# One of four chunks of a depthwise convolution, from taps on VectorE to products with tap matrices on TensorE

## The chip, the core and the metric

The kernel runs on one core of a Trainium2 chip. The metric is the device time of one execution in microseconds (us). The kernel before takes 2749.17 us (median of three runs, 2747.8 to 2751.32). The engines are named as the profile names them: PE is TensorE (its weight loads are PEld), DVE is VectorE, ACT is ScalarE, POOL is GpSimd, SP is SyncE. POOL and SP issue most DMAs here, each in its own order.

## What is computed

One step of a two-layer encoder trunk, for a prompt of 1024 frames and 8 running streams of 16 frames, 1152 columns in all, everything in fp32. Layer 0 mixes in two ways side by side: stick-breaking attention over 8 heads, and a convolution module. Only the second is touched. It takes 512 channels through a gated projection, a depthwise convolution of 31 taps over time, a layernorm over channels and a SiLU:

```python
u = a * jax.nn.sigmoid(g)
u_ext = jnp.pad(u, ((0, 0), (CONV_STATE, 0), (0, 0)))
y = lax.conv_general_dilated(u_ext, dw_w[:, None, :], window_strides=(1,), padding='VALID',
    feature_group_count=CONV_CH) + dw_b
c_out = jax.nn.silu(layernorm(y, ln_g, ln_b))
out = jnp.concatenate([a_out, c_out], axis=-1) @ w_out
```

For the running streams, the 30 cached rows of each stream stand ahead of its 16 new ones.

## The kernel before, in words

Channels lie on the 128 partitions, time in the free dimension, so that the 512 channels are four chunks (0 to 3). `mixer0` runs layer 0's mixer. `start` does the first projections; then comes a loop over four pairs of heads, p = 0 to 3, called here the first to the fourth pair. While one pair's attention runs (`attend`), the projections of the next (`proj`) fill PE, and the gate and value of a conv chunk (`ag`) stand among them: chunk 2 in the first pair, chunk 3 in the second. Chunks 0 and 1 are made in `start`.

`gate` and `value` evacuate the two projections into a tile `u` of 30 + 1024 columns for the prompt and 8 blocks of 46 for the streams. `tap(c, j)` is one of the 31 taps of chunk c: two DVE instructions, y += w[j] * u shifted by j, one over the 1024 prompt columns and one over the 128 stream columns. So there are 124 taps. `TAPS` deals them: 26 beside the first projections, 36, 38 and 24 beside the first, second and third pair. After the 31st tap a chunk is written to `cat_d` in DRAM. `conv_norm`, beside the fourth pair, loads the four chunks by column group (`yl`, three groups g of 384 columns) and does the layernorm; its mean is a product with ones (`mu`).

In `attend`, each block of 128 queries gives scores z on PE, two sigmoids on ACT (`sg`, `kp`), a scan over `kp` on DVE (L907) and a product into `sg` on DVE (L909); then PE transposes `sg` (`tpa`, L388) and multiplies with the values (`ava`). A score block is written z p i q: z217 is the third pair's second head, last query block, and sg217 the tile that follows from it.

Three lists set the order: the attention's steps with the projections by `merge` (by PE cost, with lags), the taps among them by `level` (by DVE cost), and then the framework places each engine's instructions by a cost model of its own. At run time each engine takes its instructions strictly in that order, and so do the DMA queues of SP and POOL. Where the fourth pair begins, tiles `cr` bring the attention's finished rows back from `cat_d` (SP, L1062), ACT and DVE split them into `cat`, and the output projection `psoa` reads them.

Of the kernel before, what the change touches and what calls it, by code (L numbers as in the profile page):

```python
# [15 lines left out]
P = 128  # L16
# [4 lines left out]
TAPS = (26, 36, 38, 24)  # L21
# [10 lines left out]
UW = UP + 8 * US  # L32
NF = 32
# [91 lines left out]
def tile_trunk(ctx, tc, ins, outs):  # L125
# [26 lines left out]
    dw = const.tile([P, 4, CW], F32, name="dw")  # L152
    cvec = const.tile([P, 3, 4], F32, name="cvec")
    for t, n in ((norms, "norms"), (dw, "dw"), (cvec, "cvec")):
        (nc.scalar.dma_start if n == "norms" else put)(t, ins[n])
# [23 lines left out]
    xr_d = [dram.tile([KC, P, T], F32, name=f"xr_d{l}") for l in range(2)]  # L179
    hb_d = [dram.tile([7, NF // 2, P, TW], F32, name=f"hb_d{l}") for l in range(2)]  # L180
# [474 lines left out]
    def mixer0():  # L655
        with ExitStack() as st:
# [16 lines left out]
            for p in range(4):  # L673
                mine = [p, 4 + p, 8 + p]
                if 1 <= p < 3:
                    mine[1:1] = [16 + p + 1, 12 + p + 1]
                order += mine
# [8 lines left out]
            us, ys, tapped = {}, {}, [0] * 4  # L686
            conv_pool = ExitStack()
            cv = Bufs(conv_pool.enter_context(pool("conv")), u=2, y=1)

            def gate(c, ps, g):  # L690
                if g == 0:
                    assert c < 2 or tapped[c - 2] == CW
                    us[c] = cv.tile([P, UW], F32, "u", f"u{c}")
                    nc.gpsimd.memset(us[c][:, 0:CW - 1], 0.0)
                    dma(us[c][:, UP:].rearrange("p (b t) -> p b t", t=US)[:, :, 0:CW - 1], ins["conv_in"][:, c])
# [8 lines left out]
            def u_parts(c, ps, g):  # L704
                n = G if g < 2 else TP - 2 * G
                o = CW - 1 + g * G
                parts = [(us[c][:, o:o + n], ps[:, :n], rstd[g][:, :n])]
                if g == 2:
                    parts.append((us[c][:, UP:].rearrange("p (b t) -> p b t", t=US)[:, :, CW - 1:],
                                  ps[:, n:G].rearrange("p (b t) -> p b t", t=16), None))  # L710
                return parts

            def value(c, ps, g):
                for dst, src, _ in u_parts(c, ps, g):
                    tt(dst, src, dst, ALU.mult)
                if g == 2:
                    put(outs["conv_p"][c], us[c][:, TP:UP])
                    put(outs["conv_s"][c], us[c][:, UP:].rearrange("p (b t) -> p b t", t=US)[:, :, 16:])

            def tap(c, j):  # L720
                if j == 0:
# [5 lines left out]
                          u[:, UP:].rearrange("p (b t) -> p b t", t=US)[:, :, j:j + 16]))  # L727
# [13 lines left out]
            taps = [Step(0.0, lambda c=c, j=j: tap(c, j), 1340.0) for c in range(4) for j in range(CW)]  # L741
# [220 lines left out]
            vs = pp.tile([P, 8, 2, HD], F32, "vs", "vs0")  # L962
# [3 lines left out]
            for p in range(4):  # L966
                S["p"] = p
                expand_qk(p)
                if p < 3:
                    fill = proj(p + 1)  # L970
                    if p < 2:
                        fill[10:10] = ag(p + 2)
                    n = TAPS[p + 1]
                    mix, now, taps = [], taps[:n], taps[n:]
                else:
                    cat_t = new_hs("cat0")
                    (first, fill), now = part_out(0, range(3), pp, cat_t), []
                    for s in taps:
                        s.pe = 900.0
# [987 lines left out]
```

## Time and profile before

The profiled execution took 2750.03 us, of which the span of the trace is 2748.2.

| what | value |
|---|---|
| median of three runs | 2749.17 us |
| profiled execution; its span | 2750.03 us; 2748.2 us |
| PE busy over the span | 2669.0 us, 97% |
| DVE busy over the span | 2090.5 us, 76% |
| ACT busy over the span | 1389.0 us, 51% |
| the taps (L735), 232 of their 248 instructions | 177.8 us of DVE |

The table is an average over stages with different limits. The pairs of layer 0 lie between about 95 and 545 us; what a change there is worth is read from that stretch: each engine's busy time in it, then the places where PE stands idle, and what ended the idle time.

### The profile page before, as it was taken

What the parts mean: (1) busy time and instruction counts of PE and PEld (TensorE: products, weight loads), DVE (VectorE), ACT (ScalarE), POOL (GpSimd) and SP (SyncE); (2) the same over time, 40 slices, a digit from 0 to 9 for tenths busy, and PEclk for the clock granted to TensorE, in tenths of its full rate; (3) what the DMA queues carried; (4) which work ended last, traced back from release to release, by engine and by line L of the source; (5) the groups of instructions that cost most, each with busy time, mean ns of one, the idle gap of its engine ahead of it and who ended that gap; (6) DMA issues with size and microseconds to landing.
All of it is one profiled execution on the core that took longest, in us unless ns stands there. A gap on an engine that the chain in (4) does not pass through costs nothing.

```text
span 2748.2 us, 50583 instructions
## 1 busy us (share of the span) xinstructions
PE 2669.0 (97%) x19362; PEld 2557.1 (93%) x19362; DVE 2090.5 (76%) x4117; ACT 1389.0 (51%) x2906; POOL 328.3 (12%) x599
## 2 busy tenths in 40 slices
PE   8999898999999999999999999998999999999998
PEld 8987776799999999999999999997999999999998
DVE  8999998888777755758577777778787777647577
ACT  5344456755554543435355555556555555434344
POOL 1100101041111100000011111110221111100001
PEclk9999999999999999999999999999999999999999
DMA  4434446454343377435444444446533343684344
GB/s 157 121 111 147 118 141 223 145 176 143 139 146 141 138 260 250 124 100 170 146 140 138 140 135 135 139 132 229 179 132 137 141 145 138 230 270 134 96 125 145
DMA packets 173203, 422.90 MB, mean 154 GB/s; under 512 B 25968, under 2 KB 53808, under 8 KB 170912
## 3 DMA queue, kind: packets, MB, share of 16 engines
q1 hardware_dynamic: 135696, 288.38, 33.1%
q0 software_dynamic: 37120, 131.27, 13.9%
q8 instruction: 152, 2.49, 0.4%
q14 instruction: 91, 0.75, 0.1%
q10 hardware_dynamic: 144, 0.02, 0.0%
HBM read 289.60 MB, written 117.34 MB: 148 GB/s over the span
## 4 chain that ended last, share of the span: by engine, by line
PE 76%; DVE 12%; ACT 4%; issue 4%; DMA 3%; POOL 0%; SPq 0%; DVEq 0%; ACTq 0%; POOLq 0%
PE um L1461 25%; PE pd L1686 25%; PE psc L225 10%; PE psp L225 3%; DVE y L735 3%; PE avc L467 2%; PE tpc L455 2%; DVE kp L907 2%; PE f L225 1%; PE psoa L225 1%; DMA cr<-cat_d 1%; PE zc L1201 1%; PE zc L1202 1%; PE zs L568 1%; PE so L602 1%
## 5 line engine op out<-in xcount | busy, mean ns | idle before, releaser
L225 PE MATMUL psc<-h,hl_wc 128*128 128x384 f32 x1728 | 327.2, 339 | 0.0
L225 PEld LDWEIGHTS psc<-h,hl_wc 128*128 128x128 f32 x1728 | 296.8, 188 | 13.3 <-issue 10.9
L1461 PE MATMUL um<-sl,hl_m 128*128 128x288 f32 x1548 | 240.3, 295 | 0.0
L1461 PEld LDWEIGHTS um<-sl,hl_m 128*128 128x128 f32 x1548 | 217.7, 188 | 0.0
L1686 PE MATMUL pd<-tm,hl_wd 128*128 128x288 f32 x1584 | 214.7, 294 | 0.0
L1686 PEld LDWEIGHTS pd<-tm,hl_wd 128*128 128x128 f32 x1584 | 211.3, 189 | 0.0
L735 DVE SCALAR_TENSOR_TENSOR y<-u,dw,y 128x1024 f32<-128x1024 f32 (+1 forms) x232 | 177.8, 806 | 0.6
L225 PE MATMUL psp<-h,hl_wi 128*128 128x384 f32 x864 | 165.7, 344 | 0.0
L1468 ACT ACTIVATE hdm<-hdm 128x288 f32<-128x288 f32 x192 | 84.7, 442 | 156.5 <-DVE hdm L1467 154.8
L225 PEld LDWEIGHTS psp<-h,hl_wi 128*128 128x128 f32 x864 | 150.9, 191 | 7.0 <-issue 6.2
L186 DVE TENSOR_TENSOR tm<-xr,tm 128x576 fp32r<-128x576 f32 (+1 forms) x120 | 85.8, 715 | 93.9 <-ACT tm L185 93.6
L185 ACT ACTIVATE tm<-xr 128x576 fp32r<-128x576 f32 (+1 forms) x120 | 77.6, 646 | 95.8 <-PE pd L1686 74.0
L1168 ACT ACTIVATE s<-s,mxc 128x640 f32<-128x640 f32 (+4 forms) x128 | 88.9, 694 | 60.2 <-DVE mxc L1165 58.6
L1461 PE MATMUL um<-sl,hl 128*128 128x288 f32 x756 | 119.1, 296 | 0.0
L1686 PE MATMUL pd<-th,hl_wd 128*128 128x288 f32 x792 | 113.7, 297 | 3.8 <-DVE th L186 3.7
L1686 PEld LDWEIGHTS pd<-th,hl_wd 128*128 128x128 f32 x792 | 108.2, 190 | 4.8 <-DVE th L186 4.2
L1686 PE MATMUL pd<-xr,hl_wd 128*128 128x288 f32 x792 | 112.4, 296 | 0.0
L1686 PEld LDWEIGHTS pd<-xr,hl_wd 128*128 128x128 f32 x792 | 108.0, 190 | 0.0
L1461 PEld LDWEIGHTS um<-sl,hl 128*128 128x128 f32 x756 | 106.4, 188 | 0.8
L1686 PE MATMUL pd<-tm,hl 128*128 128x288 f32 x768 | 104.9, 295 | 0.0
L1686 PEld LDWEIGHTS pd<-tm,hl 128*128 128x128 f32 x768 | 103.1, 188 | 0.0
L185 ACT ACTIVATE whc<-tpc 128x512 fp32r<-128x512 f32 (+1 forms) x144 | 72.5, 523 | 46.7 <-PE tpc L455 45.8
(526 smaller groups left out, 6637.0 us busy)
## 6 DMA issues: line engine op xcount, KB each, us to landing
xr<-hb_d SPq DMA_DIRECT2D x208, 288.0 KB, 3.0
xr<-in_w_up_dram SPq DMA_DIRECT2D x64, 512.0 KB, 4.2
hb_d<-hdm POOLq DMA_DIRECT2D x96, 288.0 KB, 2.4
hb_d<-t POOLq DMA_DIRECT2D x96, 288.0 KB, 2.4
wm<-in_w_down_dram SPq DMA_DIRECT2D x64, 256.0 KB, 4.0
st_wd<-in_w_down_dram SPq DMA_DIRECT2D x64, 256.0 KB, 3.5
st_wc<-in_w_in_c_dram SPq DMA_DIRECT2D x44, 256.0 KB, 2.9
xm_d<-xo POOLq DMA_DIRECT2D x16, 576.0 KB, 3.5
```

The source lines that it names most:

```text
L185: ACT(hi, src, AF.Copy)
L186: return tt(lo, src, f(hi), ALU.subtract)
L225: mm(ps()[:, :G], hl[:, a, at:at + P], act[g][k // 4][b][:, k % 4, :], start=n == 0, stop=n == len(todo) - 1)
L455: nc.tensor.transpose(tp[:, c0 + q * P:c0 + (q + 1) * P], blocks.get(j, tile_q), ident)
L467: mm(st["av"][:, o0:o0 + n], vs[:, j, i].rearrange("p a d -> p (a d)"), src[:, c0:c0 + n], start=st["done"] == 0, stop=st["done"] == nmm - 1)
L568: mm(box["z"][at // 512][own, at % 512:at % 512 + kw], qb[:, own], k[:, b * kw:b * kw + kw], start=True, stop=True)
L735: stt(src if j == CW - 1 else dst, src, wj, dst, ALU.mult, ALU.add)
L907: nc.vector.tensor_tensor_scan(keep[:, 0:n][:, ::-1], keep[:, 0:n][:, ::-1], ones[:, 0:1].to_broadcast([P, n]), 1.0, ALU.mult, ALU.mult)
L1168: ACT(s[:, :n], s[:, :n], AF.Exp, bias=mx, scale=-1.0, accum_out=tot)
L1461: mm(banks[b, n][:, :TQ], w[:, a, c * P:c * P + P], combo(key, c)[:, h, n * TQ:n * TQ + TQ], start=k < 3 and c == 0 and i == 0, stop=c == ...
L1468: ACT(y, y, AF.Relu)
L1686: mm(ps, w[:, a, m * P:m * P + P], b[:, h, (n - ns[0]) * TQ:(n - ns[0]) * TQ + TQ], start=first and s == 0, stop=j == NJ - 1 and s == 2, s ...
```

## The change

Chunk 3 gets no taps. `TAPS` is now 26, 26, 28 and 13, over 93 taps. Chunk 3's gate and value are moved behind all of the second pair's projections (before, they stood after the first of three), and are stored by phase: time t goes to phase t mod 8, 180 steps a phase (`UC`), so that neighbouring times lie 720 bytes apart in the tile. `value` writes the tile to DRAM (`u_d`) and makes the two cache outputs through ACT copies. In the third pair, `products` reads `u_d` back with 16 channels times 8 phases on the partitions (`ur`, in runs of 720 bytes), and for each of 8 groups of channels does 5 fp32 products of a 128x128 matrix of taps with 176 columns, accumulated in PSUM. ACT adds the bias in two instructions a group; the result goes to DRAM (`y_d`). The 40 matrices come in 20 DMAs of 128 KB by SP into the half of the tile `vs` that was unused. `conv_norm` loads chunk 3 from `y_d` in runs of 192 bytes (`yp`), and one more ACT copy a column group puts it in order.

```diff
-TAPS = (26, 36, 38, 24)
+TAPS = (26, 26, 28, 13)
...
     def gate(c, ps, g):
...
-                    us[c] = cv.tile([P, UW], F32, "u", f"u{c}")
+                    us[c] = cv.tile([P, PH * UC], F32, f"u{c % 2}", f"u{c}")
...
+                        old = staging(ins["conv_ph"], f"cp{c}", PH * 32)
+                        ACT(u[:, :, 132:].rearrange("p h (b s) -> p h b s", s=6)[:, :, :, 0:4],
+                            old[:, :PH * 32].rearrange("p (h b s) -> p h b s", h=PH, s=4), AF.Copy)
...
+                o = 4 + g * G // PH
+                parts = [(us[c][:, :, o:o + n // PH].rearrange("p h s -> p s h"),
+                          *(t.rearrange("p (s h) -> p s h", h=PH) for t in (ps[:, :n], r)))]
...
+                put(u_d, us[c])
+                new = sp.tile([P, 512], F32, "st", f"cn{c}")
...
-            taps = [Step(0.0, lambda c=c, j=j: tap(c, j), 1340.0) for c in range(4) for j in range(CW)]
+            taps = [Step(0.0, lambda c=c, j=j: tap(c, j), 1340.0) for c in range(3) for j in range(CW)]
...
+                def load():
+                    r = box["r"] = cv.tile([P, PH * UC], F32, "u1", "ur").rearrange("p (i s) -> p i s", i=PH)
+                    put(r, u_d.rearrange("(i q) h s -> (q h) i s", q=CG))
+                    for n in range(4):
+                        toeplitz(n)
+                def one(i):
...
+                    for d in range(ND):
+                        at = i * ND + d
+                        mm(ps[:, :n], toep[at // 2][:, at % 2], r[:, i, d:d + n], start=d == 0, stop=d == ND - 1)
...
+                    ACT(r[:, i, :TP // PH], ps[:, :TP // PH], AF.Identity, bias=b)
...
+                    if i == PH - 1:
+                        put(y_d.rearrange("(i q) h s -> (q h) i s", q=CG), r[:, :, :YC])
+                return ([Step(50.0, load, 0.0, "ur")]
+                        + [Step(1500.0, lambda i=i: one(i), 0.0, None, "ur", 9000) for i in range(PH)])
...
                     if p < 2:
-                        fill[10:10] = ag(p + 2)
+                        n = (10, len(fill))[p]
+                        fill[n:n] = ag(p + 2)
...
-                    mix, now, taps = [], taps[:n], taps[n:]
+                    mix, now, taps = products() if p == 2 else [], taps[:n], taps[n:]
...
-                for c in range(4):
+                for c in range(3):
                     put(box["y"][c], cat_d[0][4 + c, :, g * G:g * G + G])
+                n = G // PH
+                t = pools[0].tile([P, G], F32, "yp", f"yp{g}").rearrange("p (h s) -> p h s", h=PH)
+                put(t, y_d[:, :, g * n:g * n + n])
+                ACT(box["y"][3].rearrange("p (s h) -> p s h", h=PH), t.rearrange("p h s -> p s h"), AF.Copy)
```

How the order moves at three places. DVE at the end of the first pair, the rows that lead to its last tile sg017 (kp017 is the scan; l and q are the next pair's keys and queries; y1 and u1 are taps of chunk 1). Before:

```order
L877 TENSOR_TENSOR sv01_2101<-psp121_2110,rh0_315 128x384
L735 SCALAR_TENSOR_TENSOR y1_1239<-u1_389,dw_77,y1_1239 128x128
L735 SCALAR_TENSOR_TENSOR u1_389<-u1_389,dw_77,y1_1239 128x1024
L735 SCALAR_TENSOR_TENSOR u1_389<-u1_389,dw_77,y1_1239 128x8x16
L351 TENSOR_TENSOR l0_745<-sk01_1870,k0_743 64x1024
L907 SCALAR_TENSOR_TENSOR kp017_2126<-kp017_2126,ones_74 128x1024
L351 TENSOR_TENSOR l1_746<-sk01_1870,k1_744 64x1024
L909 TENSOR_TENSOR sg017_2125<-sg017_2125,kp017_2126 128x1023
```

Now:

```order
L770 SCALAR_TENSOR_TENSOR y1_1459<-u1_393,dw_77,y1_1459 128x1024
L952 TENSOR_TENSOR sv01_2089<-psp121_2098,rh0_319 128x384
L770 SCALAR_TENSOR_TENSOR y1_1459<-u1_393,dw_77,y1_1459 128x128
L358 TENSOR_TENSOR l1_750<-sk01_1860,k1_748 64x1024
L360 SCALAR_TENSOR_TENSOR q1_746<-sq01_1180,q1_746 64x1024
L982 SCALAR_TENSOR_TENSOR kp017_2114<-kp017_2114,ones_74 128x1024
L193 TENSOR_TENSOR hl_wi13_0_2233<-st_wi13_0_2231,hl_wi13_0_2233 128x512
L984 TENSOR_TENSOR sg017_2113<-sg017_2113,kp017_2114 128x1023
```

Between sg016 and sg017 there stood 11 tap instructions, and now there are 7; the key and query work of the next pair still stands ahead of sg017.

POOL where chunk 3's value is done (cpa and cs are attention results on their way to `cat_d`). Before:

```order
L363 DMA cat_d0_109<-cpa102_2901 64x256
L717 DMA out_conv_p_dram<-u3_2561 128x30
L718 DMA out_conv_s_dram<-u3_2561 1024x1x30
L363 DMA cat_d0_109<-cpa103_3045 64x256
L363 DMA cat_d0_109<-cpa110_3144 64x256
```

Now, at the end of the second pair:

```order
L370 DMA cat_d0_111<-cs01_3033 128x128
L752 DMA out_conv_p_dram<-cn3_3390 128x30
L746 DMA u_d_118<-u3_3013 128x1440
L753 DMA out_conv_s_dram<-cn3_3390 1024x1x30
L370 DMA cat_d0_111<-cpa112_3404 64x256
L793 DMA ur_3433<-u_d_118 128x8x180
```

The write to `u_d` and the read of `ur` are new, and an attention result stands between them. On PE the first group of products (`cv0`) stands five projection blocks of 12 products behind the last score block z117 of the second pair.

SP where the fourth pair begins (ct are cached keys and values of the streams, three buffers; the row of `vs0` is a load of tap matrices). Before:

```order
L539 DMA ct02v13_4189<-in_sb_v_dram 128x1024
L537 DMA ct03k00_4516<-in_sb_k_dram 128x4x256
L537 DMA ct03k01_4518<-in_sb_k_dram 128x4x256
L537 DMA ct03k02_4520<-in_sb_k_dram 128x4x256
L1062 DMA cr00_4450<-cat_d0_109 128x1152
L1079 DMA xo00_4703<-in_x_dram 128x3x384
L192 DMA st_wo0a5_0_5125<-in_w_out_ab_dram 128x384
L192 DMA st_wo0a6_0_5297<-in_w_out_ab_dram 128x384
L1062 DMA cr01_4467<-cat_d0_109 128x1152
L537 DMA ct03k03_4533<-in_sb_k_dram 128x4x256
```

Now:

```order
L546 DMA ct02v13_4233<-in_sb_v_dram 128x1024
L544 DMA ct03k00_4550<-in_sb_k_dram 128x4x256
L784 DMA vs0_751<-in_dw_t_dram 128x256
L199 DMA st_wo0a5_0_5161<-in_w_out_ab_dram 128x384
L544 DMA ct03k01_4552<-in_sb_k_dram 128x4x256
L1142 DMA cr00_4484<-cat_d0_111 128x1152
L544 DMA ct03k02_4554<-in_sb_k_dram 128x4x256
L1159 DMA xo00_4737<-in_x_dram 128x3x384
L544 DMA ct03k03_4567<-in_sb_k_dram 128x4x256
L1142 DMA cr01_4501<-cat_d0_111 128x1152
```

The load of cr01 now stands behind that of ct03k03, which needs the buffer of ct03k00; before it stood ahead of it.

## Rows read from the trace of the kernel before

**Rows 1.** Five stretches, busy us: length, PE, PEld, DVE, ACT, POOL; clock, DMA share, GB/s.

```profile
95.00:210.00 115.00, 112.86 (x825) 100.35 (x824) 112.61 (x149) 55.63 (x127) 10.59 (x20) 1.00 0.48 141
210.00:326.00 116.00, 105.64 (x748) 90.22 (x747) 111.75 (x152) 50.19 (x120) 12.58 (x22) 0.96 0.41 124
326.00:425.00 99.00, 91.75 (x735) 75.77 (x734) 97.61 (x126) 56.99 (x132) 10.05 (x18) 0.98 0.45 137
425.00:465.00 40.00, 30.12 (x191) 20.89 (x191) 28.08 (x51) 22.84 (x54) 5.99 (x12) 0.91 0.70 237
465.00:545.00 80.00, 75.97 (x565) 61.51 (x564) 72.26 (x134) 64.91 (x139) 7.58 (x14) 0.98 0.53 182
```

**Rows 2.** Waits of PE, 0 to 700 us: us in total, times, longest.

```profile
PE tpa L388 <- DVE sg L909: 20.2, 8, 6.2
...
PE z L924 <- DVE u L715: 1.0, 1, 1.0
...
PE z L924 <- DVE sk L877: 0.7, 1, 0.7
```

**Rows 3.** Timeline of PE behind two waits: start, length, in brackets idle before.

```profile
219.31 0.90 PE L388 MATMUL tpa<-ident,sg 128*128 128x128 f32 x3 [6.17 <-DVE sg L909]
219.86 2.46 PE L225 MATMUL psp<-h,hl_wi 128*128 128x384 f32 x7
...
226.88 2.38 PE L225 MATMUL psp<-h,hl_wi 128*128 128x384 f32 x12
...
407.28 3.47 PE L225 MATMUL psp<-h,hl_wi 128*128 128x384 f32 x12
```

**Rows 4.** Timeline of DVE ahead of the longest wait.

```profile
205.32 5.91 DVE L735 SCALAR_TENSOR_TENSOR y<-u,dw,y 128x128 f32<-128x128 f32 x8
...
214.47 2.27 DVE L907 TENSOR_TENSOR_SCAN kp<-kp,ones 128x1024 f32<-128x1024 f32 x1
...
218.03 1.23 DVE L909 TENSOR_TENSOR sg<-sg,kp 128x1023 f32<-128x1023 f32 x1
```

**Rows 5.** One DVE group by shape, 60 to 430 us: busy, mean ns of one.

```profile
L715 DVE TENSOR_TENSOR u<-psa,u 128x384 f32<-128x384 f32 x4 | 2.2, 538 | 0.0
```

**Rows 6.** PE groups by shape: busy, mean ns (pipelined), idle before.

```profile
L225 PE MATMUL psp<-h,hl_wi 128*128 128x384 f32 x864 | 165.7, 344 | 0.0
L388 PE MATMUL tpa<-ident,sg 128*128 128x128 f32 x206 | 31.9, 282 | 21.0 <-DVE sg L909 20.2 <-DVE cpa L410 0.8
...
L1021 PE MATMUL mu<-yl,ones 128*128 128x384 f32 x24 | 8.3, 490 | 0.0
...
L263 PE MATMUL ms_l<-ones,sq_l 128*128 128x1 f32 x18 | 2.3, 244 | 0.1
```

**Rows 7.** DMA issues: count, KB each, median us to landing.

```profile
xm_d<-xo POOLq DMA_DIRECT2D x16, 576.0 KB, 3.5
...
cr<-cat_d SPq DMA_DIRECT2D x10, 576.0 KB, 4.8
...
out_conv_s_dram<-u POOLq DMA_DIRECT2D x2, 120.0 KB, 6.5
```

**Rows 8.** Timelines at the turn to the fourth pair, of PE, DVE, ACT, SP.

```profile
418.88 0.39 PE L925 MATMUL z<-l,q 128*128 128x512 f32 x1
...
429.67 1.03 PE L388 MATMUL tpa<-ident,sg 128*128 128x128 f32 x6 [4.14 <-DVE sg L909]
433.27 0.69 PE L225 MATMUL psoa<-cat,hl_wo0a 128*128 128x384 f32 x1 [2.57 <-ACT cat L185]
...
423.56 1.22 DVE L351 TENSOR_TENSOR l<-sk,k 64x1024 fp32r<-64x1024 f32 x1
...
432.69 1.35 ACT L185 ACTIVATE cat<-cr 128x384 fp32r<-128x384 f32 x3 [1.84 <-DMA cr<-cat_d]
441.36 1.35 ACT L185 ACTIVATE cat<-cr 128x384 fp32r<-128x384 f32 x3 [2.30 <-DMA cr<-cat_d]
...
434.77 0.33 SPq L1062 DMA_DIRECT2D cr<-cat_d  x1
```

More of the change, by code (lines that the diff above doesn't have):

```diff
@@ L32 @@
 UW = UP + 8 * US
+PH = 8
+UC = 180
+YC = T // PH
+CG = 16
+ND = 5
 NF = 32
@@ L151, in tile_trunk @@
     norms = const.tile([P, 5, KC], F32, name="norms")
-    dw = const.tile([P, 4, CW], F32, name="dw")
+    dw = const.tile([P, 3, CW], F32, name="dw")
+    dwb = const.tile([P, PH], F32, name="dwb")
     cvec = const.tile([P, 3, 4], F32, name="cvec")
-    for t, n in ((norms, "norms"), (dw, "dw"), (cvec, "cvec")):
+    for t, n in ((norms, "norms"), (dw, "dw"), (cvec, "cvec"), (dwb, "dwb")):
         (nc.scalar.dma_start if n == "norms" else put)(t, ins[n])
@@ L179, in tile_trunk @@
     xr_d = [dram.tile([KC, P, T], F32, name=f"xr_d{l}") for l in range(2)]
+    u_d, y_d = (dram.tile([P, PH, n], F32, name=f"{t}_d") for t, n in (("u", UC), ("y", YC)))
     hb_d = [dram.tile([7, NF // 2, P, TW], F32, name=f"hb_d{l}") for l in range(2)]
@@ L961, in mixer0 @@
             qs, kd, kl = ([ep.tile([P, TP], F32R, f"{n}{i}", f"{n}{i}") for i in range(2)] for n in "qkl")
-            vs = pp.tile([P, 8, 2, HD], F32, "vs", "vs0")
+            both = pp.tile([P, 2048], F32, "vs", "vs0")
+            vs = both[:, :1024].rearrange("p (j h d) -> p j h d", j=8, h=2)
+            mats = both[:, 1024:].rearrange("p (n m) -> p n m", m=P)
             run(level(proj(0), taps[:TAPS[0]]))
@@ L977, in mixer0 @@
                     (first, fill), now = part_out(0, range(3), pp, cat_t), []
-                    for s in taps:
-                        s.pe = 900.0
-                    mix = taps + conv_norm(lambda: (conv_pool.close(), Bufs(st.enter_context(pool("ln")), t1=3, yl=5))[1],
-                                           cat_t)
+                    mix = conv_norm(lambda: (conv_pool.close(), Bufs(st.enter_context(pool("ln")), t1=3, yl=5))[1],
+                                    cat_t)
                 cat = Cat(0, p, wk, cat_t)
@@ L1913, in _lay_out @@
     o["norms"] = n.reshape(5, 8, 128).transpose(2, 0, 1)
-    o["dw"] = a["dw_w"][0].reshape(31, 4, 128).transpose(2, 1, 0)
+    w = a["dw_w"][0].reshape(31, 4, 128)
+    o["dw"] = w[:, :3].transpose(2, 1, 0)
+    w = w[:, 3].reshape(31, 8, 16)
+    m = np.zeros((8, 5, 16, 8, 16, 8), w.dtype)
+    for d in range(5):
+        for pi in range(8):
+            for po in range(8):
+                if 0 <= 8 * d + pi - po - 2 < 31:
+                    for c in range(16):
+                        m[:, d, c, pi, c, po] = w[8 * d + pi - po - 2, :, c]
+    o["dw_t"] = m.reshape(20, 2, 128, 128).transpose(0, 2, 1, 3).reshape(20, 128, 256)
+    o["dwb"] = np.repeat(a["dw_b"][0][384:].reshape(8, 16), 8, axis=1).transpose(1, 0)
     v = np.stack([a["dw_b"][0], a["conv_ln_g"][0], a["conv_ln_b"][0]])
     o["cvec"] = v.reshape(3, 4, 128).transpose(2, 0, 1)
-    o["conv_in"] = a["cache_conv"][0].reshape(8, 30, 4, 128).transpose(3, 2, 0, 1)
+    w = a["cache_conv"][0].reshape(8, 30, 4, 128).transpose(3, 2, 0, 1)
+    o["conv_in"] = w[:, :3]
+    w = np.concatenate([np.zeros((128, 8, 2), w.dtype), w[:, 3]], axis=2)
+    o["conv_ph"] = w.reshape(128, 8, 4, 8).transpose(0, 3, 1, 2).reshape(128, 256)
     o["sb_k"] = a["cache_sb_k"][0].reshape(8, 1024, 4, 128).transpose(2, 0, 3, 1)
```

61 lines of the change are left out of this document (49 added, 12 removed).

## The prediction

> **What bounds the kernel now.** I read busy time by stage first. Over the first three pairs of heads (95 to 425 us) DVE is busy 112.6 of 115, 111.8 of 116 and 97.6 of 99 us, PE 112.9, 105.6 and 91.8 [rows 1]. Both are nearly full, DVE fuller. In the fourth pair (465 to 545 us), which has no taps, DVE is busy 72 of 80 and PE still misses 4 [rows 1]. So the second thing to read is who ends PE's idle time: the transposes wait for the tile `sg` from DVE 8 times, 20.2 us in all, longest 6.2 [rows 2], and 0.8 us for another DVE result [rows 6]; scores wait 1.0 and 0.7 us for DVE [rows 2]. Of these 22.7 us, 4.14 lie at the turn to the fourth pair [rows 8], which I take apart below; 18.6 us lie in the three pairs. Third, what stands ahead of the longest wait on DVE: eight tap instructions in 5.91 us, then the scan and the product that PE waits for [rows 4]. DVE runs late because of the taps, and PE pays where a pair ends. Fourth, what a wait leaves behind: after 6.17 us of idling PE needs 2.30 us for 7 products (219.86 to 222.16), where 12 take 2.38 later on [rows 3]. The granted clock averages 0.96 and 0.98 in these two stages [rows 1]: it falls from 2.4 to 1.2 GHz during a wait and comes back a few us later.
>
> So the taps are not worth their own time, only what PE waits for them, and the change buys that with new work on the engine that would be next.
>
> **Part one, taps taken away.** A tap is two instructions; eight stand in 5.91 us, so one tap costs 1.48 [rows 4]. The first three pairs lose 10, 10 and 11 taps: 14.8, 14.8 and 16.3 us of DVE. Per stage that is more than the waits there, so DVE's sum leaves the bound: 98, 97 and 81 us against PE's 113, 106 and 92 without its idle time. Whether a wait goes is decided locally, by what stands ahead of the tile. At the end of the first pair there are still 7 tap instructions instead of 11 between sg016 and sg017, and the next pair's key and query work. In the new order PE has 36 projection products (0.192 each, 6.9 us [rows 6]) and some 2.7 us of transposes and small products, together about 9.6 us, between the last score block and the transpose of sg017; DVE has about 11.4 us between sg016 and sg017 (seven tap instructions 4.9, scan 2.27, product 1.23 [rows 4], keys and queries 2.4, two small ones 0.6), and starts on it about 1.5 us before the score block. That is an estimate, and it leaves 0.3 to 2.3 us of the 6.17; I keep 1.3. The other ends of pairs come out with no wait by the same count. I leave another 1.0 us for waits that I can't place, like those of the fourth pair. Gain 16.3 us; bounds 9 (half of it stays) and 18.6.
>
> **Part two, the clock.** If 1.0 minus the granted clock were all lost work, 116 x 0.04 + 99 x 0.02 = 6.6 us [rows 1]; part of it falls into the idle time and costs nothing. Two places that I can time lost 0.9 us (7 products in 2.30 for 1.39) and 1.1 us (12 in 3.47 for 2.38) [rows 3]. Between 2.0 and 6.6 I take 4, since there are about four such places.
>
> **Part three, products added.** 40 fp32 products of a 128x128 matrix with 176 columns, each shown as two records: 80 records on PE, all on the path, since PE is then the bound. No such shape is in the trace. One-pass products of 384 columns cost 165.7/864 = 0.192 us each, the fp32 records of 384 columns 8.3/24 = 0.346, and those of one column 2.3/18 = 0.128 [rows 6]. The second pass adds 0.154 per 384 columns and some 0.038 is fixed, so 176 columns in two passes cost 0.141 + 0.038 = 0.179, and 80 of them 14.3 us. Bounds: in proportion to the columns of `mu` 0.159, 12.7 us; on the line from one column to 384 0.228, 18.2 us. I take 14.3, because its two rows are the same engine in the same state.
>
> **Part four, the way through DRAM.** PE takes its instructions in order, so if `ur` isn't there when cv0 is next, everything behind it waits. Counted from the last score block of the second pair: DVE's scan starts about 4 us later, as at the third pair's end (keys begin 4.3 us after the score block ends [rows 8]); scan, product and two value instructions (2.27 + 1.23 + 0.54 x 2, [rows 4, 5]) end at about 8.6. The write of 737 KB by the row of 576 KB is 3.5 x 737/576 = 4.5 us, the read back 4.8 x 737/576 = 6.1 [rows 7]; with some half a us for each of two issues the data are there at 20. PE has 60 projection products (11.5 us) and 19 transposes (0.155 each, 2.9) [rows 6], and some 3 us of small products ahead of cv0: 17.4. So PE waits 2 to 3 us once; I take 2. Bounds: 0 (transfers no slower than the rows of 576 KB), and 8 (both as slow as the 6.5 us of small runs [rows 7], with their size on top). The matrices come in four buffers by SP; the shortest distance between two groups is some 4 us of PE work for a load of 128 KB, so I count them at nothing.
>
> The phase-wise gate and value write single elements 720 bytes apart. Their eight DVE instructions replace as many of 0.54 or less [rows 5], and no row shows such a step. From nothing to fourfold they add 0 to 12 us of DVE in the second pair, which has been relieved of 14.8; up to about 9 is hidden by DVE's new slack (97 against PE's 106). I take nothing. What the Trainium skill says, in SBUF — State Buffer, "Door 1: The DMA port swizzle", speaks against this: it describes lines of 16 bytes, and a penalty for each access that goes to a new line. No run here shows it. By that page these eight would be the slow kind, and at twofold price (an estimate from the page's rule) the sum would not move.
>
> **Part five, the turn to the fourth pair.** Before, z217 ends at 419.27, PE waits 4.14 us for sg217 and 2.57 for `cat`, and the first `psoa` is at 433.27, 14.0 us later; `cr` arrives 7.9 us after the key work that frees its buffer (423.56 + 1.22 to 432.69), the second `cr` is issued at 434.77 and arrives 6.6 us on [rows 8]. Now one tap less stands ahead of the key work, and the first `cr` comes 1.5 us earlier, or up to 4.6 if it takes the usual 4.8 [rows 7]: 3 taken. The second `cr` stands behind ct03k03, which needs PE to be done with ct03k00: 2.2 us later. Net 0.8 us earlier, and the last group of products (1.8 us) lies inside the wait. Gain 2.5 us, between a loss of 2 and a gain of 4.
>
> The chunk's own load `yp` has runs of 192 bytes and an ACT copy behind it, which holds up ACT until it lands. The nearest row is 6.5 us for runs of 120 bytes, against 4.8 of `cr` [rows 7]; in the new order ACT waits for the second `cr` just ahead of it, which is issued later, so it is hidden. The Trainium skill, DMA: Bandwidth & Descriptors, "Specifications", puts the smallest transfer at full rate at 512 bytes. The row of 6.5 us agrees with that; by this rule alone the copy would cost 2 us more, once.
>
> **The sum.** -16.3 - 4 + 14.3 + 2 - 2.5 = -6.5 us. It is made in the profiled execution (2750.0, its span 2748.2), 0.9 over the median; I take it off the median: 2749.2 - 6.5 = 2743. By the bounds alone it could be 2732 or 2766, but not all ends come together.
>
> **The rivals.**
> *The waits belong to the order, not to the sum; slower.* sg017 waits behind keys, queries and scan in any case, and PE also missed 4 of 80 us in the fourth pair where DVE has 10% to spare [rows 1]. If only 9 of 18.6 us come back, 2 us of clock, the products cost their upper 18.2 and the turn gains nothing, it is -9 - 2 + 18.2 + 2 = +9: 2758. It decides from less than about half of the waits recovered. Against it: in the first stage PE misses only 2.1 of 115 us, although DVE is as full [rows 1]: the waits come from a backlog that grows, not from each tile.
> *The round trip; no change.* cv0 waits 8 us instead of 2, the clock falls behind it as after the 6.17 us wait (0.9 us): 2743 + 7 = 2750. For it: two transfers in a row behind a POOL queue that waits for attention results. Against: five blocks of projections stand ahead.
> *All of it comes back.* -18.6 - 6 + 12.7 - 3 = -15: 2734. For it speaks DVE's slack of 10% and more in each stage.
> *The stride.* At fourfold price the second pair's 12 us exceed the slack by 3, which come back as waits, with a us of clock: 2747. The SBUF page named above is the rule for this; nothing in the trace bears it out.
>
> **How the numbers follow.** Chances: the forecast 0.46 (2738 to 2749), all of it 0.13, round trip 0.20, stride 0.05, slower 0.16. What a measurement of this kernel can tell from no change is about 0.2%, 5.5 us: faster is below 2743.7, slower above 2754.7. Of the forecast somewhat over half is below 2743.7 and most of the rest between: faster 0.27 + 0.13 and some of the others, 0.45; slower 0.16 and the far end of the round trip, 0.19; same 0.36. The range for 8 in 10 goes from 2735 to 2757: it takes in most of the fast rival and the nearer half of the slow one.
>
> **What would show it.** Waits of PE for `sg` in the three pairs fall from 16 us to about 3, and the granted clock there to 0.99 or more; DVE's share falls to about 90%; 80 records at 0.16 to 0.20 us each; one wait of cv0 for `ur` of 0 to 4 us; the first `psoa` 9 to 13 us after z217. I am wrong if waits for `sg` stay at over 8 us, if products cost over 0.22 us a record, if cv0 waits over 6 us, or if the time moved outside 95 to 470 us.

## The result: slower, by more than the range allowed

The changed kernel takes 2761.3 us (median of 5 runs, 2757.0 to 2768.3) against 2750.8 for the kernel before on the same chip; the ratio is 1.004, interval 1.0025 to 1.0054. That is 10.5 us slower where 6.5 us faster was forecast, and outside the range. The profiled execution of the changed kernel is the fastest of its five (2757.0, span 2755.2), so its trace shows 7.0 us of the loss and hides the rest.

First the same stretches as in [rows 1], from the trace of the changed kernel (length, then busy us of PE, PEld, DVE, ACT, POOL; clock, DMA share, GB/s):

```profile
95.00:210.00 115.00, 112.68 (x832) 100.24 (x830) 107.87 (x137) 55.48 (x129) 11.74 (x22) 1.00 0.51 147
210.00:326.00 116.00, 110.52 (x805) 95.65 (x805) 102.09 (x131) 55.34 (x127) 9.75 (x18) 0.97 0.42 124
326.00:425.00 99.00, 94.79 (x727) 81.51 (x728) 73.92 (x95) 55.77 (x137) 11.84 (x20) 0.97 0.53 158
425.00:465.00 40.00, 30.64 (x171) 20.68 (x169) 21.48 (x39) 21.29 (x49) 7.09 (x11) 0.87 0.74 237
465.00:545.00 80.00, 75.70 (x552) 59.83 (x551) 72.16 (x133) 63.38 (x140) 7.47 (x13) 0.96 0.54 179
```

DVE has slack now (102 of 116, 74 of 99 us), as meant. But the clock hardly differs in the first three stretches (1.00, 0.97 and 0.97, before 1.00, 0.96 and 0.98), and it is lower in the fourth (0.87, before 0.91), where PE is idle for a quarter of the time in both kernels. Which waits are left, 0 to 700 us of the changed kernel (us in total, times, longest):

```profile
PE tpa L395 <- DVE sg L984: 10.2, 5, 3.5
PE psoa L232 <- ACT cat L192: 7.9, 3, 4.0
...
PE cv L803 <- DMA ur<-u_d: 1.8, 1, 1.8
```

The waits for `sg` fell from 20.2 [rows 2] to 10.2 us, and less of that was won in the pairs than it seems. Of the 20.2 us 4.14 lay at the turn [rows 8]; there is no wait for `sg` there now, but the wait for `cat` right behind it grew from 2.57 to 4.04. In the three pairs the waits for `sg` fell from 16.1 to 10.2 us, and all waits for DVE from 18.6 to 10.2. At the turn PE waits for `cat` three times, before 2.57 [rows 8], 0.76 and 1.68 us (the next fence), 5.0 together, and now 7.9.

Where the time goes is seen by laying rows of PE with the same work side by side. The kernel before (start, length, idle before in brackets), at the last score block of the second pair, that of the third, the second and third group of `psoa` that waits for a `cr` (between these two `zs`, scores of the running streams behind a wait for `qb`), and a product of the MLP behind them:

```profile
326.06 0.22 PE L927 MATMUL z<-maskd,unit 128*128 128x128 f32 x1
...
419.11 0.22 PE L927 MATMUL z<-maskd,unit 128*128 128x128 f32 x1
...
441.94 2.44 PE L225 MATMUL psoa<-cat,hl_wo0a 128*128 128x384 f32 x12 [0.76 <-ACT cat L185]
...
451.75 0.64 PE L568 MATMUL zs<-ct03k,qb 128*32 128x256 f32 x8 [0.66 <-ACT qb L559]
...
456.69 3.48 PE L225 MATMUL psoa<-cat,hl_wo0a 128*128 128x384 f32 x18 [1.68 <-ACT cat L185]
...
609.70 0.53 PE L1461 MATMUL um<-t2m,hl_m 128*128 128x288 f32 x2 [1.31 <-ACT hl_m L185]
```

The changed kernel, the same places, with its waits between them:

```profile
316.20 0.22 PE L1002 MATMUL z<-maskd,unit 128*128 128x128 f32 x1
...
327.38 1.75 PE L395 MATMUL tpa<-ident,sg 128*128 128x128 f32 x7 [3.50 <-DVE sg L984]
...
342.03 1.73 PE L803 MATMUL cv<-ur,vs 128*128 128x176 f32 x10 [1.84 <-DMA ur<-u_d]
...
419.87 0.22 PE L1002 MATMUL z<-maskd,unit 128*128 128x128 f32 x1
...
431.19 0.44 PE L232 MATMUL psoa<-cat,hl_wo0a 128*128 128x384 f32 x1 [4.04 <-ACT cat L192]
...
443.97 0.44 PE L232 MATMUL psoa<-cat,hl_wo0a 128*128 128x384 f32 x1 [2.46 <-ACT cat L192]
...
455.53 1.00 PE L575 MATMUL zs<-ct03k,qb 128*32 128x256 f32 x8 [0.66 <-ACT qb L566]
...
461.78 3.47 PE L232 MATMUL psoa<-cat,hl_wo0a 128*128 128x384 f32 x18 [1.43 <-ACT cat L192]
...
616.64 0.53 PE L1541 MATMUL um<-t2m,hl_m 128*128 128x288 f32 x2 [1.04 <-ACT hl_m L192]
```

Four stretches come out of it. Up to the last score block of the second pair the change wins 9.9 us (326.06 to 316.20). From there to that of the third pair it loses 10.6 (93.05 before, 103.67 after): the products stand here. From there to the first `psoa` it wins 2.8 (14.16 before by [rows 8], 11.32 after). From the first `psoa` to the MLP it loses 9.0 (176.43 before, 185.45 after). Together +6.9, and next to nothing is added behind it (the spans differ by 7.0). The forecast had no loss in the last stretch at all.

The products and the phase-wise multiplication are priced by two groups of the changed kernel, of PE over the four pairs and of DVE from 300 to 330 us (busy us, mean ns of one; products overlap, so the price of one on PE is busy time by count):

```profile
L803 PE MATMUL cv<-ur,vs 128*128 128x176 f32 x80 | 13.6, 316 | 1.8 <-DMA ur<-u_d 1.8
```

```profile
L739 DVE TENSOR_TENSOR u<-psa,u 128x384 f32<-128x384 f32 x2 | 1.9, 942 | 0.0
```

80 records at 0.170 us, as forecast (0.179). A phase-wise multiplication of 384 columns costs 0.94 us, against 0.54 for the contiguous one [rows 5].

At the turn, SP of the changed kernel (issues of the `cr` loads and of their neighbours):

```profile
422.53 0.47 SPq L1142 DMA_DIRECT2D cr<-cat_d  x1
...
436.29 0.37 SPq L544 DMA_DIRECT2D ct03k<-in_sb_k_dram  x1
436.89 0.34 SPq L1142 DMA_DIRECT2D cr<-cat_d  x1
...
454.82 0.34 SPq L1142 DMA_DIRECT2D cr<-cat_d  x1
```

The second `cr` goes out 2.1 us later than before (434.77 [rows 8]), because a load of `ct03k` that waits for PE stands ahead of it.

### The profile page after: what moved, and what is told of

Read it like the earlier page. It is cut to its first block, busy times and chain, and to the rows that moved or that the text cites. A ratio compares the mean times of both kernels' runs of the same rounds, so it can differ in the third digit from the quotient of the medians.

```text
span 2755.2 us, 50747 instructions
## 1 busy us (share of the span) xinstructions
PE 2683.7 (97%) x19442; PEld 2571.7 (93%) x19442; DVE 2052.7 (75%) x4055; ACT 1397.7 (51%) x2928; POOL 331.3 (12%) x601
## 4 chain that ended last, share of the span: by engine, by line
PE 69%; DVE 4%; DMA 2%; ACT 2%; issue 1%; DVEq 0%; ACTq 0%; SPq 0%
PE um L1541 25%; PE pd L1766 25%; PE psc L232 10%; PE avc L474 2%; PE tpc L462 2%; PE zc L1281 1%; PE zc L1282 1%; PE psoa L232 1%; DMA st_wo1b<-in_w_out_c_dram 1%; PE so L609 1%; PE zs L575 1%; DMA cr<-cat_d 0%; DVE xr L1447 0%; ACT s L1248 0%; DVE sl L1771 0%
## 5 line engine op out<-in xcount | busy, mean ns | idle before, releaser
L770 DVE SCALAR_TENSOR_TENSOR y<-u,dw,y 128x128 f32<-128x128 f32 (+1 forms) x174 | 133.9, 806 | 0.7
L982 DVE TENSOR_TENSOR_SCAN kp<-kp,ones 128x128 f32<-128x128 f32 (+3 forms) x64 | 86.4, 1350 | 14.4 <-ACT kp L1004 13.9
```

The costliest lines, as they stand in the source:

```text
L770: stt(src if j == CW - 1 else dst, src, wj, dst, ALU.mult, ALU.add)
L982: nc.vector.tensor_tensor_scan(keep[:, 0:n][:, ::-1], keep[:, 0:n][:, ::-1], ones[:, 0:1].to_broadcast([P, n]), 1.0, ALU.mult, ALU.mult)
```

## The experiments

Times are medians of runs. Each group of experiments ran beside the kernel before, whose median lay between 2750.4 and 2753.0, so the ratio to before stands with each time. The ratios are taken over all runs of both kernels and are not quotients of the two medians, so a difference by ratios can be a few us off from one by medians; between experiments of different groups the ratio is the safer measure. After stands for the changed kernel.

**x1_taps_only: what the taps are worth alone.**

```
-            TAPS = (26, 36, 38, 24)          +  TAPS = (26, 26, 28, 13)
-   taps ... for c in range(4) ...            +  taps ... for c in range(3) ...
+   if c == 3: put(cat_d[0][7], u)            (value: the gated chunk goes out as it is)
```

> The kernel before with the 31 taps of the fourth chunk left out and nothing put in their place (the gated chunk goes to DRAM as it is, so its output is not the convolution); taps dealt 26, 26, 28, 13 and the chunk's projections at the end of the second pair, as in the changed kernel. It prices part one by itself. If the waits for sg come from DVE's sum over a stage, about 16 of 18.6 us come back with 4 us of clock: 2727 to 2732, waits for sg in the three pairs 1 to 4 us. If they come from what stands ahead of each pair's last tiles in DVE's order, the changed kernel's trace tells the price: 8 to 9 us of waits come back and 8 to 10 us of waits for sg stay, 2736 to 2742.

2732.3 us, ratio 0.993 (0.9913 to 0.9946): 19.2 us faster than before. PE's waits for `sg` in it:

```profile
PE tpa L388 <- DVE sg L914: 9.5, 5, 3.2
```

Both theories were half right. The time is all but that of the sum (2732), the waits left are those of the order: 9.5 us of waits for `sg` stay, 8.2 of them in the three pairs, at four of the five places that have them in the changed kernel, and 1.3 at the turn. So in the three pairs 10.4 of the 18.6 us of waits for DVE came back. Nor do all of the 19 us belong to the pairs: at the last score block of the third pair the trace is 15.3 us ahead of before (403.80 against 419.11), and the other 3 of its 18.5 us lie behind it. What is not waits I can't split further. The recovered time is real, so something else in the change spends almost 30 us.

**x2_no_products: the changed kernel without its 40 products.**

```
-  mm(ps[:, :n], toep[at // 2][:, at % 2], r[:, i, d:d + n], ...)
+  pass                                     (ACT copies r in place instead of ps)
```

> The changed kernel without the 40 products: the tiles that they would read are copied in place by ACT and written to DRAM, so the fourth chunk is not convolved; taps, phases, matrices' loads and the way through DRAM stay. If the products lie wholly on PE's path, as the trace says (80 records, 13.6 us busy), it is 13 to 16 us faster than the changed kernel: 2745 to 2748, near the kernel before. If part of them only fills time in which PE would wait at the turn anyway, less than 10 us. If the turn's loss (6 us) comes from the products' place in the order, it goes too: 2739 to 2742.

2742.2 us, ratio 0.9965 (0.9953 to 0.9978): 19.1 us faster than after, more than the 13.6 us that the products are busy. The trace says where. Between the last score blocks of the second and the third pair, where the products stood, x2 is only 5.1 us shorter than after (314.46 to 413.03, 98.57). From the first `psoa` to the MLP it is 9.2 us shorter (424.93 to 601.21, 176.28), as short as before. So the turn's loss went with the products, the third case of the expectation: without them the planner issues the second `cr` at 426.43, ahead of the next `ct03k` (428.82), and no wait for the second or third `cr` is left. Against x1 it is 10 us slower: that is the price of the rest, the way through DRAM above all. Here ACT takes the wait for `ur`, and PE gets it at second hand. ACT's timeline:

```profile
344.19 0.40 ACT L808 ACTIVATE ur<-ur,dwb 128x128 f32<-128x128 f32 x1 [11.17 <-DMA ur<-u_d]
```

and PE's, 4 us later:

```profile
348.15 0.80 PE L580 MATMUL zn<-kn,qb 128*128 128x128 f32 x2 [6.55 <-DVE cpa L417]
```

**x3_no_yp: the chunk read back in rows.**

```
-  put(t, y_d[:, :, g * n:g * n + n])       (runs of 192 bytes into yp)
-  ACT(box["y"][3]..., t..., AF.Copy)
+  put(box["y"][3], y_d.rearrange("p h s -> p (h s)")[:, g * G:g * G + G])
```

> The changed kernel with the fourth chunk read back in rows as it lies in DRAM (its tokens are then in the wrong order): no runs of 192 bytes, no ACT copy. If the turn's 6 us come from this load and its copy, 4 to 6 us faster than the changed kernel, and the wait for the second cr is 1 us or less. If they come from the second cr's place on SP behind ct03k03, or from the clock behind the waits, it is within 2 us of the changed kernel and PE still waits 2 to 3 us for the second cr.

2759.2 us, ratio 1.0022 (1.0012 to 1.0032): 2.1 us faster than after by the medians, 5 by the ratios, and the intervals overlap, so the time alone doesn't decide. The trace does: PE still waits 2.77 us for the second `cr`, and the scores `zs` come 23.2 us after the first `psoa` (434.08 to 457.27), against 24.3 in after and 18.5 before. So the load and its copy are not the turn's loss, or about 1 us of it. The trace shows another thing. Up to the first product it does the same as after, and yet PE waits 3.9 us longer there:

```profile
343.26 3.27 PE L803 MATMUL cv<-ur,vs 128*128 128x176 f32 x10 [5.70 <-DMA ur<-u_d]
...
447.24 0.85 PE L232 MATMUL psoa<-cat,hl_wo0a 128*128 128x384 f32 x3 [2.77 <-ACT cat L192]
...
463.99 5.99 PE L232 MATMUL psoa<-cat,hl_wo0a 128*128 128x384 f32 x18 [3.46 <-ACT cat L192]
```

The 1.84 us in the trace of after are the shortest of the four traces with the same instructions ahead of this wait (x8 1.99, x4 2.58, x3 5.70). For what this load costs, the prediction had an estimate of 2 us by a rule of the Trainium skill (DMA: Bandwidth & Descriptors, "Specifications": full rate from 512 bytes on). The 2.1 us of the medians would agree with it, the 5 us of the ratios would not, and these runs can't tell the two apart.

**x4_cr_buffer: a buffer of its own for the second cr.**

```
-  cr = pp.tile([P, T], F32, "sk", ...)
+  cr = spare if spare is not None and c == 1 else pp.tile([P, T], F32, "sk", ...)
   (spare = both[:, 1024:], the half that the matrices leave free, 2176 columns instead of 2048)
```

> The changed kernel with a buffer of its own for the second cr (the free half of the tile that holds the values and the matrices), which puts its load right behind the first cr on SP, ahead of three loads of ct03k. If the turn is lost by the second cr's place on SP, PE's wait for it (2.46 us) goes, the clock in 425 to 465 us rises from 0.87 to about 0.91, and it is 3 to 6 us faster than the changed kernel. If it is lost by the chunk's own load and copy, or by DMA traffic as a whole, at most 1 us faster, and the first cr lands later by as much as the second lands earlier.

2754.9 us, ratio 1.0006 (0.9995 to 1.0017): 6.4 us faster than after by the medians, 9 by the ratios, whose intervals don't overlap. On SP the two loads now stand together (`vs` is the buffer):

```profile
422.27 0.47 SPq L1142 DMA_DIRECT2D cr<-cat_d  x1
422.97 0.33 SPq L1142 DMA_DIRECT2D vs<-cat_d  x1
```

PE doesn't wait for the second `cr` any more, and the scores `zs` come 19.4 us after the first `psoa`, against 24.3 in after and 18.5 before. PE of x4:

```profile
430.75 0.69 PE L232 MATMUL psoa<-cat,hl_wo0a 128*128 128x384 f32 x1 [3.86 <-ACT cat L192]
...
450.17 0.64 PE L575 MATMUL zs<-ct03k,qb 128*32 128x256 f32 x8 [0.66 <-ACT qb L566]
```

The clock in 425 to 465 us did not rise (0.87), so that part of the expectation fell.

**x7_before_cr_buffer: the same buffer in the kernel before** (the same diff).

> The kernel before with the same buffer of its own for the second cr. Before, its load stood ahead of the loads of ct03k on SP already, and PE waited 0.76 us for it. If x4 won by undoing what the change did to the order, this gains nothing here: 2749 to 2752. If any kernel gains by an earlier second cr, it gains 3 us or more: under 2748.

2753.7 us, ratio 1.0002 (0.9992 to 1.0013): nothing. So x4 won by mending what the change had done to the order, or by the earlier load that goes with it; x12 below tells these apart.

**x5_deal and x6_early: the waits for sg that are left.** Both start from x4.

```
x5   -  TAPS = (26, 26, 28, 13)             +  TAPS = (26, 26, 20, 21)
x6   -  ... < at / pe * dve:                +  ... < min(1.0, at / pe / 0.85) * dve:
```

> x4_cr_buffer with eight taps moved from the second pair to the third (26, 26, 20, 21 instead of 26, 26, 28, 13). In x4 PE waits 6.0 us for sg in the second pair (0.91, 1.62, 3.48), where DVE is busy 103 of 116 us, and 0.98 in the third, where it is busy about 80%. If the sum over a stage decides, DVE at 92 of 116 leaves at most 1 us of the 6: 2749 to 2751. If what stands ahead of the last tiles decides, the stretch behind the last but one tile loses two of its seven tap instructions, 1.5 to 2.5 us of waits go in the second pair and up to 2 come in the third: 2753 to 2756.

> x4_cr_buffer with the same number of taps in each pair, dealt over the first 85% of the pair's work, so that none stands ahead of its last tiles; the sum over a stage doesn't change. If the waits for sg that are left (9.2 us in three pairs) are a matter of the order ahead of the last tiles, 5 to 8 us of them go: 2747 to 2751. If they are a matter of the sum, or if the taps that stand closer together now make waits earlier in the pair, the waits only move, within 2 us of x4: 2753 to 2757.

x5: 2753.1 us, ratio 1.0004 (0.9993 to 1.0015), within 2 us of x4. x6: 2758.6 us, ratio 1.0019 (1.0006 to 1.0031), if anything slower. Yet in both the wait for `sg` at the end of the second pair, 3.48 us in x4, did what its theory said. PE of x5:

```profile
323.43 0.98 PE L395 MATMUL tpa<-ident,sg 128*128 128x128 f32 x7 [0.71 <-DVE sg L984]
...
341.27 3.27 PE L803 MATMUL cv<-ur,vs 128*128 128x176 f32 x10 [7.51 <-DMA ur<-u_d]
```

and of x6, where that place has no wait at all (the first row is an earlier one of the second pair):

```profile
296.75 1.51 PE L395 MATMUL tpa<-ident,sg 128*128 128x128 f32 x6 [3.90 <-DVE sg L984]
...
340.71 3.27 PE L803 MATMUL cv<-ur,vs 128*128 128x176 f32 x10 [5.98 <-DMA ur<-u_d]
```

So the time that DVE gives back before the third pair is taken again some 15 us later by the first product, which waits for the way through DRAM (2.58 us in x4). That was a new theory: PE waits first for `sg` and then for `ur`, which comes by a write and a read that start behind the same tile on DVE, and mending the first wait alone brings little. How the time was lost between the two, POOL shows for x4:

```profile
327.87 0.54 POOL L746 DMA_DIRECT2D u_d<-u  x1
...
331.71 0.93 POOL L793 DMA_DIRECT2D ur<-u_d  x1 [1.37 <-DMA u_d<-u]
```

and for x5:

```profile
325.58 0.54 POOL L746 DMA_DIRECT2D u_d<-u  x1
...
333.14 0.93 POOL L793 DMA_DIRECT2D ur<-u_d  x1 [5.08 <-DMA u_d<-u]
```

Counted from the first transposes of `sg` (at 116.97 us in x4, 119.24 in x5), x5 issues the write 4.6 us earlier, but its write takes 7.3 us and that of x4 3.6, and so the first product comes only 1.2 us earlier. x6 issues the write 1.3 us earlier, its read takes 10.2 us and that of x4 8.3, and the first product comes 0.6 us later. In these traces it was thus a longer transfer that took the gain, not the order alone; why it was longer stays open. x6 also has a wait of 3.90 us where x4 has one of 0.91: with the taps closer together, a part of the waits only moved.

**x9_late, x10_late_deal, x11_late_early: the products begin later.** The same edit on x4, x5 and x6:

```
-  [Step(1500.0, lambda i=i: one(i), 0.0, None, "ur", 9000) for i in range(PH)]
+  [Step(1500.0, lambda i=i: one(i), 0.0, f"cv{i}", f"cv{i - 1}" if i else "ur",
+        6000 if i else 16000) for i in range(PH)]
```

> x4_cr_buffer with the products begun some 6 us of PE work later in the third pair and spread over the rest of it; nothing else is changed. In x4 PE waits 2.6 us for ur at the first product, and up to 7.5 in runs of its kin. If the way through DRAM is what holds PE there, that wait goes: 2749 to 2752, and the times of single runs lie closer together than the 9 us of x4. If the wait only moves (to the matrices, which four buffers now bring later, or to the next scores), within 1.5 us of x4's 2755.

> x5_deal with the same later products. In x5 the wait for sg at the end of the second pair fell from 3.5 to 0.7 us, and the wait for ur grew from 2.6 to 7.5: if the two are one and the same, because the transfer begins at a fixed point of DVE's order, then only both edits together bring time, 6 to 8 us against x4: 2746 to 2749. If the dealing alone is worth nothing, as x5 showed, and the wait for ur was a matter of chance, it is the same as x9.

> x6_early with the same later products. In x6 no wait for sg was left at the ends of the first two pairs, and the wait for ur was 6.0 us. If that wait was all that took the gain back, 2746 to 2750; if the taps that stand closer together cost by themselves (3.9 us of a wait for sg in the second pair), 2752 to 2756.

| | taps as in after | dealt anew (x5) | early (x6) |
|---|---|---|---|
| products as in after | 2754.9, 1.0006 | 2753.1, 1.0004 | 2758.6, 1.0019 |
| products later | 2751.1, 0.9998 (0.9985 to 1.001) | 2743.7, 0.9964 (0.9951 to 0.9976) | 2745.3, 0.9981 (0.9966 to 0.9996) |

Against x4, the dealing alone brings 1.8 us, the later products alone 3.8, both together 11.2 (by the ratios 0.5, 2 and 11.5). Early dealing alone loses 3.7, and with the later products it wins 9.6 (by the ratios 3.6 and 7). In both columns the pair brings more than its parts, by about 0.3% of the time; the four intervals combined (the root of the sum of their squares) leave some 0.25% open. That is clear, but not by much, and both columns rest on x4 and x9, so they are not two independent signs. Between the transposes of the last `sg` of the second pair and the first product PE has 10.3 us of work and a wait of 7.5 in x5; in x10 it has 19.4 us of work and no wait:

```profile
317.92 0.98 PE L395 MATMUL tpa<-ident,sg 128*128 128x128 f32 x7 [0.69 <-DVE sg L985]
...
337.35 1.65 PE L803 MATMUL cv<-ur,vs 128*128 128x176 f32 x10
```

None of x9 to x12 has a wait for `ur`. That this wait is what ate the gain of the dealing in x5 and x6 is the likeliest reading, argued from the four times and not seen in one trace.

One expectation fell: the single runs of x9 lie 8 us apart (2746.7 to 2754.8), hardly closer than those of x4 (9 us). The kernel before, which has neither the way through DRAM nor products, scatters by 15 us beside x9 (25 runs, 2745.8 to 2760.8). So the runs scatter without that wait too; by what stays open. The profiled execution of x10 is also its fastest (2736.1 of 2736.1 to 2748.7), so its trace flatters it.

**x8_held: two groups of products moved into the wait at the turn** (on x4).

```
+  mix, held = mix[:-2], mix[-2:]           (third pair)
+  if p == 3: run(held)                     (ahead of the fourth pair)
```

> x4_cr_buffer with the last two of the eight groups of products held back until behind the third pair's last small products, where PE waits 3.9 us for the first cr. If that wait is free for products, it is 2 to 4 us faster than x4, 2751 to 2753, and the wait for the first cr falls under 1 us. Against it: the chunk's result goes to DRAM some 5 us later and its read back with it, so the means wait for it; then it is within 1 us of x4 or up to 3 us slower.

2766.6 us, ratio 1.0052 (1.0033 to 1.0071): 11.7 us slower than x4. Neither case of the expectation. The wait was not free: the last matrices now come in the middle of the turn's loads (issued at 428.25, there 9 us later). The chunk's write to `y_d` goes out at 439.62 us, in x4 at 425.34; on POOL the loads `yl` of the other chunks wait 5.1 us for it, and the means wait for them. PE of x8:

```profile
437.21 1.54 PE L803 MATMUL cv<-ur,vs 128*128 128x176 f32 x4 [2.45 <-DMA vs<-in_dw_t_dram]
...
447.62 1.62 PE L1104 MATMUL mu<-yl,ones 128*128 128x384 f32 x2 [2.34 <-DMA yl<-cat_d]
```

**x12_late_deal_no_buffer: x10 without the buffer.** With the new dealing and the later products the planner puts the second `cr` ahead of the fourth `ct03k` again, so two causes of x4's gain, the place and the buffer, can be told apart.

> x10_late_deal without the second cr's own buffer: the changed kernel with only the dealing (26, 26, 20, 21) and the later products. With these the planner has the second cr ahead of the fourth load of ct03k on SP, as in the kernel before. If the turn was lost by that place on SP, the buffer isn't needed any more: within 2 us of x10, 2742 to 2746, and PE waits under 1 us for the second cr. If the buffer itself won x4's 6 us, by loading early, they are missing here: 2748 to 2751.

2742.8 us, ratio 0.9965 (0.9951 to 0.9979), the same as x10, and PE has no wait for the second `cr`. SP of x12:

```profile
427.24 0.34 SPq L1143 DMA_DIRECT2D cr<-cat_d  x1
429.34 1.67 SPq L544 DMA_DIRECT2D ct03k<-in_sb_k_dram  x2
```

So the place on SP is enough, and the buffer isn't needed. x12 is the changed kernel with two edits, its table of taps and the times of its products, and beats both kernels: 8 us faster than before, 18 than after.

## Why the prediction was wrong, step by step

| Term | Forecast | Measured |
|---|---|---|
| one and two, taps and clock | -20.3 | -15.3 to the end of the third pair's scores, -19.2 in all, when alone (x1); in the whole change it doesn't stay |
| one, waits for DVE, three pairs | 18.6 to 2.3 | 18.6 to 10.2 (trace of after), 8.2 (x1) |
| two, clock in the second and third stage | 0.99 or more | 0.97 and 0.97 |
| three, products | +14.3 | 13.6 busy; without them their stretch is 5.1 shorter (x2) |
| four, way through DRAM | +2, bounds 0 and 8 | 1.84 in the trace of after; 2.6 to 7.5 in x3 to x6; with strides and `yp` about 10 (x1 to x2) |
| five, the turn | -2.5 | -2.8 to the first `psoa`, then +9.0 to the MLP, of which x4 gets back 5.1 in its trace (6.4 by the medians) |

**The likeliest case** named the right bound. Right too were the products' price, the first `psoa` 9 to 13 us after the third pair's last scores (11.3), and the second `cr`'s delay on SP (2.2 us forecast, 2.1 measured). Of its own signs of being wrong one came: waits for `sg` over 8 us. The time did not move outside 95 to 470 us for the most part; 5.1 of the 6.9 us had come by 461.78.

**The step that failed most** is part five. It saw the second `cr` behind `ct03k`, gave it 2.2 us, and set that against the 3 us by which the first `cr` comes earlier. But the two don't cancel: the first one's gain ends at the first `psoa`, and the loss begins behind it. Counted from the first `psoa`, the group that waits for the second `cr` comes 4.1 us later than before, the scores `zs` 5.9, the products behind the third `cr` 7.2, the MLP 9.0. Only 1.7 us of this are PE's longer wait for the second `cr` (0.76 to 2.46); behind it `psoa`, `mu` and the third `cr` stand one behind the other on PE, ACT and SP. The trace misses the forecast by 13.5 us (7.0 slower instead of 6.5 faster), and 9.0 of them lie in this stretch, which the forecast had at nothing. x4 and x12 show the place on SP as the cause of about half of it or more; x7 excludes that any kernel gains by the buffer, x2 and x3 that the chunk's own load is to blame. Of the 9.0 us 3.9 are left in x4's trace (430.75 to 611.11) and 4.7 in that of x12 (425.74 to 606.90); I didn't take them apart.

**Part one** was too large. Alone, the taps brought 15.3 us up to the last scores of the third pair where parts one and two had 20.3. It counted, tile by tile, that the waits at the ends of pairs would go. At the end of the first pair 3.1 us stayed instead of 1.3. The two lengths it counted there were right (DVE 11.7 us for 11.4, PE 9.8 for 9.6), but DVE began on them 1.0 us behind the end of the score block and not 1.5 ahead of it. At the end of the second pair 3.5 us stayed instead of nothing. Some of DVE's rows between the last two tiles there, from the trace of the changed kernel:

```profile
319.98 0.96 DVE L739 TENSOR_TENSOR u<-psa,u 128x384 f32<-128x384 f32 x1
...
321.20 1.22 DVE L358 TENSOR_TENSOR l<-sk,k 64x1024 fp32r<-64x1024 f32 x1
322.45 1.22 DVE L360 SCALAR_TENSOR_TENSOR q<-sq,q 64x1024 fp32r<-64x1024 f32 x1
323.71 2.29 DVE L982 TENSOR_TENSOR_SCAN kp<-kp,ones 128x1024 f32<-128x1024 f32 x1
```

Taps, one phase-wise multiplication and the next pair's keys and queries stand ahead of the scan. The price of the stride was left at nothing; it is 1.7 times the contiguous one [rows 5], near the twofold that the prediction tried out. The Trainium skill's page SBUF — State Buffer ("Door 1: The DMA port swizzle"), with a penalty for each access to a new 16-byte line, has the sign right, and this trace agrees with it. That the waits left are in good part a matter of order, x6 shows: with the same number of taps in each pair the ones at the ends of the first two pairs are gone, and those in the three pairs fall from 10.1 (x4) to 6.6 us, with the 3.90 among them.

**Part four** had the mechanism, and its 2 us came out in the trace of after (1.84) by luck. Counted from the end of the second pair's last score block (316.42), it had the scan at 4 us, the values done at 8.6, `ur` there at 20 and PE at the first product at 17.4. In the trace these are 7.3, 12.3, 25.6 and 23.8: the transfer came 5.6 us late, and PE 6.4 us late, 3.5 of them because it had waited for the same scan. The transfers were priced too low as well, at 4.5 us to write and 6.1 to read, from rows of contiguous transfers [rows 7]. (The 737 KB there are thousands of bytes and the 576 KB are of 1024; in one unit, 720 to 576, it is 4.4 and 6.0.) The eleven traces with this way have 3.6 to 7.5 for the write and 8.0 to 10.2 for the read.

It also took parts one and four as two sums that add up. Both hang on the same tile of DVE: PE waits for `sg`, and later for the transfer that starts behind it. Dealing the taps anew brought 1.8 us while PE waited for that transfer (x4 to x5), and 7.4 once it did not (x9 to x10). The rival of the round trip thus named a real cost, 2 to 4 us by x9, but not the largest one.

**The slower rival** (2758) came nearest in time, by sums that were partly others: over half of the waits for DVE did stay, but the products were not at their upper price, and the turn did not gain nothing, it lost 6 net (2.8 won, 9.0 lost). Its chance, 0.16, was too low above all because no case had the turn lose more than 2 us, though every edit ahead of it moves the planner's order there.

**The account of the measured 10.5 us**, by single edits: taps alone -19.2 (x1); what remains without products +10.0 (x1 to x2: way through DRAM, strides, `yp` and copies); the products with the turn's order +19.1 (x2 to after, which ran in different groups). Sum +9.9; the rest is the 0.6 us between the medians of before. The last term can't be split into products and turn by adding: the products are busy 13.6 us, but without them PE waits in their stretch instead, and there only 5.1 us came back.

## What to carry to other kernels

Relieving a full engine is worth what its consumer waits for, but a wait that stands further on can take the gain again; here two edits that brought 1.8 and 3.8 us alone brought 11.2 together, so test pairs of edits before giving one up. Where a planner or a queue in order deals the instructions, a change in one stage can move a load behind a waiting one in the next: read the queue's order at the next stage and price everything that stands behind the load, not only its own wait. One profiled execution can be the best of its kind, so a wait on DMA is priced from several traces.

## What the runs showed of the hardware that was not expected

- In the eleven traces with the same two transfers, the write of 720 KB to DRAM took 3.6 us in one kernel and 7.5 in another (x4, x2), the read back 8.0 to 10.2 (x5, x3). With the same instructions ahead of it, PE's wait behind them was 1.84 to 5.70 us (after, x3).
- The 18 products behind the third `cr` took 3.47 us behind a wait of 1.43 (after), at a granted clock of 1.00, but 5.99 behind 3.46 (x3), at 0.52, which is the lower level of 1.2 GHz nearly throughout. That stretch of x3 (columns as in the first fence):

```profile
464.00:469.90 5.90, 5.90 (x18) 5.61 (x18) 3.51 (x11) 4.03 (x7) 0.00 (x0) 0.52 0.03 10
```

  It is not the length of the last wait alone: in x12 they took 5.03 us behind 2.03 (clock 0.66), in x10 3.47 behind 3.39 (clock 1.00). Nor is it the number of waits ahead: from the first `psoa` on, PE had waited for `mu` and `cat` four times in x12 and twice in x10, but only once in x4, where they took 4.93 us behind 2.85 (clock 0.66). What decides stays open.
